# A two-layer decoder trunk on one core: the k-tiles of tokens and of z moved from 2048 to 2080 bytes apart

## The chip, the cores and the metric

The kernel runs as one launch on one core of a Trainium2 chip. The metric is the device time of that launch in microseconds. Three runs of the kernel before took 821.86, 821.97 and 822.0 us; the median is 821.97 us.

## The reference

Two layers work on a sequence of 256 positions (T) of width 2048 (D). Everything that costs time is a product with a large fp32 weight matrix:

```python
for i in range(2):
    if i == 1:
        k_blocks, v_blocks, k_mean = moba_shared_kv(h, w_kv_shared)   # h @ (2048 x 3072)
    u = h @ w_in[i]                                                    # 2048 x 4096
    branch_in, gate_b, mem_q, gate_m = jnp.split(u, split_at, axis=-1)
    branch = multiscale_pool(...) if i == 0 else moba_attention(...)
    mem_o = memory_attention(mem_q, mem, w_mem_kv[i])                  # mem @ (2048 x 1024), 4 heads
    mixed = jnp.concatenate([branch * silu(gate_b), mem_o * silu(gate_m)], -1)
    h = layer_norm(DEEPNORM_ALPHA * h + mixed @ w_out[i], ln_g[i], ln_b[i])
```

The sequence is one attention block long, so the attention of layer 1 is plain causal attention over 12 heads of 128.

## The kernel before, in words

Each fp32 operand is held as two fp32r parts, a high one and a low one (`split`, L69 to L72: ScalarE copies to the high part, VectorE subtracts to get the low part). A product is high x high + high x low + low x high. All matmuls go through `mm` (L66, L67), so nearly all of them carry L67 in the profile, and they are told apart by the names of their tiles. In the profile's names the tile before the comma or after it may be either operand; which one streams (moving) and which one is loaded into the array (weights of the array, "stationary") is told here.

The activations stand transposed, with the 2048 channels cut into 16 k-tiles of 128 partitions. One k-tile of a transposed activation is 512 numbers per partition: 256 positions of the high part, then 256 of the low part, 2048 bytes in all. Three such tensors stay in the on-chip memory: `xT` (the tokens, later the output of layer 0), `memT` (the memory tokens) and `zT` (the gated branches, "z"). `xT` and `memT` lie in one large tile `xm`, `memT` right behind `xT`, both moved up by `SHIFT` = 40 numbers (160 bytes) from the start of the tile (L55 to L57). `zT` is a tile of its own that begins with its first k-tile (L59).

Weight matrices arrive as 128 x 1024 blocks (`raw`, 4 buffers) on SP's DMA queue, and each is split into `wh` and `wl` (4 buffers each, 4096 bytes per partition). A list of items, one for each block, is worked off in order by `run` (L130 to L164): at item i the block i+4 is loaded, the block i+3 is split, and the matmuls of item i are issued. There are two forms of projection.

`proj_t` (L167 to L191) makes a transposed result. The weight block is the array's operand, in slices of 128 numbers (512 bytes), and the k-tile of `xT` or `memT` streams past it: 512 columns against the slice of `wh`, then 256 columns (the high part alone) against the slice of `wl`. For each k-tile there is thus one pair of matmuls.

`proj_n` (L193 to L217) makes a result with positions on the partitions. Here 128 positions of the k-tile are the array's operand, and 512 columns of the weight block stream: the high part against `wh`, the high part against `wl`, the low part against `wh`. It is used for the memory values (`mem_v`, with `memT`), the shared values (`w_sv`, with `xT`) and the output projections (`out_0`, `out_1`, with `zT`).

Some weight blocks are split into parts of `xm` that are no longer needed. The blocks of `w_sv` go to where `memT` stood (`in_mem`, L650), so they too begin 160 bytes into a multiple of 512. The last 512 columns of the second output projection go to `kept` (L58), which is laid over `xm` without the shift, and `last` (L731) multiplies `zT` by them: 512 columns for the first 128 positions, twice 256 columns for the others. `pool_mix` (L563) streams 256 columns of `zT` past slices of a small weight block.

The addresses modulo 512 bytes follow from the shapes. `xm` (66,048 bytes per partition), `zT`, `res`, `raw`, `wh` and `wl` all have sizes that are multiples of 512 and stand behind one another, and slices of the weight blocks begin at multiples of 512 in them. Take the distance as the start of what streams minus the start of the array operand that is loaded during it, modulo 512 bytes. Before the change it is 160 in `proj_t`, 352 in `mem_v` (the array operand is 160 ahead), and 0 in `w_sv`, the output projections, `last` and `pool_mix`.

The results of `proj_t` for heads and gates pass through a small tile `fold` (L223 to L245, 3 buffers): ScalarE copies one half of the sum, VectorE adds the other, and the tile is free when VectorE's L229 (heads) or L242 (gates, one item later) has read it.

Of the kernel before, what the change touches and what calls it, by code (L numbers as in the profile page):

```python
# [11 lines left out]
F32 = mybir.dt.float32  # L12
F32R = mybir.dt.float32r
# [4 lines left out]
P = 128  # L18
T = 256
D = 2048  # L20
KT = D // P
# [11 lines left out]
BLK = 1024  # L33
RAW_BUFS = 4
WARM = 10
SHIFT = 40
W_BUFS = 4
SHIFT = 40
LD = 4
LEAD = 3  # L40
LD0 = 8
# [4 lines left out]
def trunk(ctx: ExitStack, tc: tile.TileContext, a: dict, out: bass.AP):  # L46
    nc = tc.nc
    ctx.enter_context(tc.manual_schedule())
    sb = ctx.enter_context(tc.tile_pool(name="sb", bufs=1))
# [2 lines left out]

    xm = sb.tile([P, 2 * KT * 2 * T + 128], F32R, name="xm")  # L55
    KX = KT * 2 * T
    xT, memT = (xm[:, SHIFT + i * KX:SHIFT + (i + 1) * KX].rearrange("p (k t) -> p k t", k=KT) for i in range(2))  # L57
    kept = [xm[:, i * KX:(i + 1) * KX].rearrange("p (k n) -> p k n", k=KT) for i in range(2)]  # L58
    zT = sb.tile([P, KT, 2 * T], F32R, name="zT")  # L59
    res = sb.tile([P, 2, D], F32, name="res")  # L60
    ident = mask = psc = eps_t = stats = None

# [29 lines left out]
    def later(n, fn):  # L92
        events[now[0] + n].append(fn)
# [6 lines left out]
    def load(it):  # L100
        for c0, c1 in zip(it["cuts"], it["cuts"][1:]):
            load_piece(it, c0, c1)
# [15 lines left out]
    def prep(it):  # L118
        for c0, c1 in zip(it["cuts"], it["cuts"][1:]):
            prep_piece(it, c0, c1)  # L120
# [9 lines left out]
    def run():  # L130
# [15 lines left out]
        for i in range(n):  # L146
            now[0] = i
            if i + LP < n:
                prep(items[i + LP])
            if LD0 <= i + LD < n:  # L150
                load(items[i + LD])
            it = items[i]
# [66 lines left out]
    def fold(dst, acc):  # L219
        nc.scalar.activation(dst, acc[:, T:], AF.Copy)  # L220
        nc.vector.tensor_add(dst, acc[:, :T], dst)  # L221

    def to_heads(dst, base):  # L223
        def done(n, acc):
            s = sb.tile([P, T], F32, name="fold", bufs=3)
            hi, lo = dst()[:, base + n, :T], dst()[:, base + n, T:]
            fold(s, acc)
            nc.vector.tensor_copy(hi, s)
            nc.vector.tensor_sub(lo, s, f(hi))  # L229
        return done  # L230

    def to_gate(dst, base):

        def done(n, acc):
            s = sb.tile([P, T], F32, name="fold", bufs=3)
            fold(s, acc)
            g = dst()

            def finish():
                th = sb.tile([P, T], F32, name="th", bufs=2)  # L240
                nc.scalar.activation(th, s, AF.Tanh, scale=0.5)
                nc.vector.scalar_tensor_tensor(g[:, base + n, :], th, 1.0, s,  # L242
                                               op0=ALU.add, op1=ALU.mult)
            later(1, finish)
        return done  # L245
# [6 lines left out]
    def heads_tile(name):  # L252
        return sb.tile([P, 4, 2 * T], F32R, name=name)
# [202 lines left out]
    def fresh(key, make):  # L456

        tiles = []

        def g():  # L460
            if not tiles:
                tiles.append(make())
                st[key] = tiles[0]
            return tiles[0]
        return g
# [183 lines left out]

    def in_mem(j):  # L650

        return [memT[:, 4 * (j % 4) + 2 * i:4 * (j % 4) + 2 * i + 2].rearrange("p k n -> p (k n)") for i in range(2)]

    mem_q_gate(1)
    for grp in range(3):
        k = fresh("k", lambda: heads_tile("kk"))
        q = fresh("q", lambda: heads_tile("qq"))
        g = fresh("g", gate_tile)
        v = fresh("v", val_tile)
        for c in range(2):  # L660
            proj_t(xT, [a["w_sk"][2 * grp + c, kb] for kb in range(4)], to_heads(k, 2 * c))
        for c in range(2):
            proj_t(xT, w_in(1, 2 * grp + c), to_heads(q, 2 * c))
        prs = [MobaPair(2 * j, 4 * grp + 2 * j, st) for j in range(2)]

        def go(prs=prs):
            plan(prs[0], 1, 5, 17)
            plan(prs[1], 7, 18, 20)
        after(go)
        for c in range(2):  # L670
            proj_t(xT, w_in(1, 6 + 2 * grp + c), to_gate(g, 2 * c))
        proj_n(xT, [a["w_sv"][grp, kb] for kb in range(8)], to_values(v), place=in_mem)
# [189 lines left out]
```

## Time and profile before

| | us |
|---|---|
| median of 3 runs | 821.97 |
| profiled execution, its own time | 822.53 |
| its span, first to last instruction | 820.8 |
| PE busy (matmul) | 810.8 |
| PEld busy (weight load) | 700.9 |
| DVE busy | 558.5 |
| ACT busy | 396.2 |

The page's 40 slices show PE at nine tenths or more in every slice but the last, and the granted TensorE clock the same way (mean 0.995 of full speed). A busy PE is not a PE at its peak: matmuls overlap, so the mean time of one is longer than the distance from one start to the next. The distance between starts is what adds up to the span, and it is read from the timeline.

### The profile page before, as it was taken

What the parts mean: (1) busy time and instruction counts of PE and PEld (TensorE: products, weight loads), DVE (VectorE), ACT (ScalarE), POOL (GpSimd) and SP (SyncE); (2) the same over time, 40 slices, a digit from 0 to 9 for tenths busy, and PEclk for the clock granted to TensorE, in tenths of its full rate; (3) what the DMA queues carried; (4) which work ended last, traced back from release to release, by engine and by line L of the source; (5) the groups of instructions that cost most, each with busy time, mean ns of one, the idle gap of its engine ahead of it and who ended that gap; (6) DMA issues with size and microseconds to landing.
All of it is one profiled execution on the core that took longest, in us unless ns stands there. A gap on an engine that the chain in (4) does not pass through costs nothing.

```text
span 820.8 us, 11537 instructions
## 1 busy us (share of the span) xinstructions
PE 810.8 (99%) x4446; PEld 700.9 (85%) x4446; DVE 558.5 (68%) x794; ACT 396.2 (48%) x578; POOL 0.2 (0%) x4
## 2 busy tenths in 40 slices
PE   9999999999999999999999999999999999999996
PEld 6888888898888888888888888888888888888885
DVE  5786678657956555797667667576765667658746
ACT  6564545545545343545455445354554445545520
POOL 0000000000000000000000000000000000000000
PEclk9999999999999999999999999999999999999998
DMA  8876545456557655676554544645455554636742
GB/s 319 298 250 206 170 154 192 172 181 212 185 190 278 221 186 199 201 234 201 185 170 143 193 162 163 212 159 189 177 173 170 185 187 158 224 113 233 277 132 103
DMA packets 47164, 159.15 MB, mean 194 GB/s; under 512 B 5375, under 2 KB 7167, under 8 KB 46847
## 3 DMA queue, kind: packets, MB, share of 16 engines
q1 hardware_dynamic: 45792, 155.21, 56.3%
q10 hardware_dynamic: 1316, 3.19, 1.0%
q8 instruction: 35, 0.57, 0.3%
q14 instruction: 21, 0.17, 0.1%
HBM read 156.28 MB, written 2.10 MB: 193 GB/s over the span
## 4 chain that ended last, share of the span: by engine, by line
PE 98%; DVE 1%; DMA 1%; SPq 0%; ACT 0%; issue 0%; DVEq 0%
PE acc L67 89%; PE o L67 4%; PE s L67 2%; PE pt L67 2%; DMA raw<-in_w_mk 1%; PE pt L362 0%; PE pt L312 0%; SPq L98 0%; DVE res L805 0%; PE o L637 0%; PE pt L637 0%; DVE res L786 0%; DVE wl L72 0%; ACT wh L71 0%; DVE stats L744 0%
## 5 line engine op out<-in xcount | busy, mean ns | idle before, releaser
L67 PE MATMUL acc<-xm,wh 128*128 128x512 f32 x1344 | 466.8, 394 | 0.5 <-ACT wh L71 0.5
L72 DVE TENSOR_TENSOR wl<-raw,wh 128x1024 fp32r<-128x1024 f32 (+2 forms) x250 | 295.0, 1187 | 149.8 <-ACT wh L71 148.8
L67 PE MATMUL acc<-xm,wl 128*128 128x256 f32 x1344 | 362.6, 280 | 0.1
L71 ACT ACTIVATE wh<-raw 128x1024 fp32r<-128x1024 f32 (+2 forms) x250 | 255.5, 1028 | 188.5 <-PE acc L67 131.2
L67 PEld LDWEIGHTS acc<-xm,wh 128*128 128x128 f32 x1344 | 247.2, 188 | 49.1 <-ACT wh L71 1.0
L67 PEld LDWEIGHTS acc<-xm,wl 128*128 128x128 f32 x1344 | 252.7, 188 | 7.9 <-DVE wl L72 0.9
L67 PE MATMUL acc<-wh,zT 128*128 128x512 f32 x448 | 140.0, 390 | 0.0
L67 PEld LDWEIGHTS acc<-wh,zT 128*128 128x128 f32 x448 | 84.1, 188 | 17.3
L67 PE MATMUL acc<-wl,zT 128*128 128x512 f32 x224 | 87.2, 389 | 0.0
L67 PE MATMUL acc<-xm 128*128 128x512 f32 x288 | 65.8, 389 | 0.0
L67 PEld LDWEIGHTS acc<-xm 128*128 128x128 f32 x288 | 54.1, 188 | 11.2
L72 DVE TENSOR_TENSOR xm<-raw,xm 128x1024 fp32r<-128x1024 f32 (+2 forms) x41 | 47.8, 1171 | 21.1 <-ACT xm L71 21.1
L220 ACT ACTIVATE fold<-acc 128x256 f32<-128x256 f32 x72 | 27.7, 385 | 60.8 <-PE acc L67 59.6
L71 ACT ACTIVATE xm<-raw 128x1024 fp32r<-128x1024 f32 (+2 forms) x41 | 41.3, 1014 | 19.1 <-PE acc L67 9.8
L67 PEld LDWEIGHTS acc<-wl,zT 128*128 128x128 f32 x224 | 42.1, 188 | 8.5
L221 DVE TENSOR_TENSOR fold<-acc,fold 128x256 f32<-128x256 f32 x72 | 29.5, 419 | 4.6 <-ACT fold L220 4.6
L71 ACT ACTIVATE zT<-zf 128x256 fp32r<-128x256 f32 x32 | 12.9, 414 | 39.6 <-DVE zf L282 35.4
L67 PE MATMUL acc<-xm,zT 128*128 128x256 f32 (+1 forms) x144 | 22.6, 318 | 0.0
L67 PEld LDWEIGHTS acc<-xm,zT 128*128 128x128 f32 x144 | 20.7, 190 | 1.9
L67 PE MATMUL acc<-wh,xm 128*128 128x512 f32 x64 | 21.6, 403 | 0.0
L71 ACT ACTIVATE ph<-pt 128x384 fp32r<-128x384 f32 (+1 forms) x20 | 10.7, 535 | 22.2 <-PE pt L362 13.5
L72 DVE TENSOR_TENSOR zT<-zf,zT 128x256 fp32r<-128x256 f32 x32 | 12.9, 423 | 9.7 <-ACT zT L71 9.7
(124 smaller groups left out, 504.4 us busy)
## 6 DMA issues: line engine op xcount, KB each, us to landing
raw<-in_w_in SPq DMA_DIRECT2D x128, 512.0 KB, 3.5
raw<-in_w_out SPq DMA_DIRECT2D x64, 512.0 KB, 4.1
raw<-in_w_sk SPq DMA_DIRECT2D x24, 512.0 KB, 4.4
raw<-in_w_sv SPq DMA_DIRECT2D x24, 512.0 KB, 3.3
raw<-in_w_mv SPq DMA_DIRECT2D x14, 512.0 KB, 5.2
raw<-in_w_mk SPq DMA_DIRECT2D x12, 512.0 KB, 3.4
raw<-in_xT SPq DMA_DIRECT2D x4, 512.0 KB, 4.8
res<-in_x ACTq DMA_DIRECT2D x2, 1024.0 KB, 5.4
```

The lines of the kernel that those rows point to most:

```text
L67: nc.tensor.matmul(o, l, r, start=start, stop=stop)
L71: nc.scalar.activation(hi, src, AF.Copy)
L72: nc.vector.tensor_sub(lo, src, f(hi))
L220: nc.scalar.activation(dst, acc[:, T:], AF.Copy)
L221: nc.vector.tensor_add(dst, acc[:, :T], dst)
```

## The change

The k-tiles of `xT`, `memT` and `zT` are `KP` = 520 numbers (2080 bytes) apart, with 8 unused numbers behind each. The start of k-tile k thus moves on by 32 bytes modulo 512 with each k, so the 16 k-tiles begin at the 16 multiples of 32 bytes. `xm` grows by 1024 bytes per partition, `zT` by 512. `in_mem` is given its own view, `inmem`, of unbroken 4096-byte blocks that begins where `memT` begins; `kept` stays. Both uses of `fold` get 2 buffers in place of 3. A second definition of `SHIFT` goes.

```diff
-SHIFT = 40
 W_BUFS = 4
 SHIFT = 40
+KP = 2 * T + 8
...
-    xm = sb.tile([P, 2 * KT * 2 * T + 128], F32R, name="xm")
     KX = KT * 2 * T
-    xT, memT = (xm[:, SHIFT + i * KX:SHIFT + (i + 1) * KX].rearrange("p (k t) -> p k t", k=KT) for i in range(2))
+    xm = sb.tile([P, 2 * KX + 384], F32R, name="xm")
+    at = [SHIFT + i * KT * KP for i in range(2)]
+    xT, memT = (xm[:, c:c + KT * KP].rearrange("p (k t) -> p k t", k=KT)[:, :, :2 * T] for c in at)
+    inmem = xm[:, at[1]:at[1] + KX].rearrange("p (b n) -> p b n", n=BLK)
     kept = [xm[:, i * KX:(i + 1) * KX].rearrange("p (k n) -> p k n", k=KT) for i in range(2)]
-    zT = sb.tile([P, KT, 2 * T], F32R, name="zT")
+    zT = sb.tile([P, KT, KP], F32R, name="zT")[:, :, :2 * T]
...
     def to_heads(dst, base):
...
-            s = sb.tile([P, T], F32, name="fold", bufs=3)
+            s = sb.tile([P, T], F32, name="fold", bufs=2)
...
     def to_gate(dst, base):
...
-            s = sb.tile([P, T], F32, name="fold", bufs=3)
+            s = sb.tile([P, T], F32, name="fold", bufs=2)
...
     def in_mem(j):
...
-        return [memT[:, 4 * (j % 4) + 2 * i:4 * (j % 4) + 2 * i + 2].rearrange("p k n -> p (k n)") for i in range(2)]
+        return [inmem[:, 2 * (j % 4) + i] for i in range(2)]
```

## Rows read from the trace of the kernel before

**Rows 1.** The page's first part: busy time of each engine, share of the span, instructions.

```profile
span 820.8 us, 11537 instructions
PE 810.8 (99%) x4446; PEld 700.9 (85%) x4446; DVE 558.5 (68%) x794; ACT 396.2 (48%) x578; POOL 0.2 (0%) x4
```

**Rows 2.** The page's fourth part: the chain of work that ended last, its shares of the span by engine and by line.

```profile
PE 98%; DVE 1%; DMA 1%; SPq 0%; ACT 0%; issue 0%; DVEq 0%
PE acc L67 89%; PE o L67 4%; PE s L67 2%; PE pt L67 2%; DMA raw<-in_w_mk 1%; PE pt L362 0%; PE pt L312 0%; SPq L98 0%; DVE res L805 0%; PE o L637 0%; PE pt L637 0%; DVE res L786 0%; DVE wl L72 0%; ACT wh L71 0%; DVE stats L744 0%
```

**Rows 3.** The groups of instructions, shapes kept apart, PE's matmuls: line, engine, operation, tiles, shape, count | busy us, mean ns of one | idle before. `xm,wh` and `xm,wl` are `proj_t`; `wh,zT` and `wl,zT` the output projections; `xm` alone is `w_sv`; `wh,xm` and `wl,xm` (on acc, pt and o) are `mem_v`; `xm,zT` is `last`.

```profile
L67 PE MATMUL acc<-xm,wh 128*128 128x512 f32 x1344 | 466.8, 394 | 0.5 <-ACT wh L71 0.5
L67 PE MATMUL acc<-xm,wl 128*128 128x256 f32 x1344 | 362.6, 280 | 0.1
...
L67 PE MATMUL acc<-wh,zT 128*128 128x512 f32 x448 | 140.0, 390 | 0.0
L67 PE MATMUL acc<-wl,zT 128*128 128x512 f32 x224 | 87.2, 389 | 0.0
...
L67 PE MATMUL acc<-xm 128*128 128x512 f32 x288 | 65.8, 389 | 0.0
...
L67 PE MATMUL acc<-wh,xm 128*128 128x512 f32 x64 | 21.6, 403 | 0.0
...
L67 PE MATMUL acc<-wl,xm 128*128 128x512 f32 x32 | 12.6, 393 | 0.0
L67 PE MATMUL acc<-xm,zT 128*128 128x256 f32 x96 | 11.7, 283 | 0.0
...
L67 PE MATMUL pt<-wh,xm 128*128 128x512 f32 x32 | 11.4, 396 | 0.0
L67 PE MATMUL o<-wh,xm 128*128 128x512 f32 x32 | 11.4, 396 | 0.0
L67 PE MATMUL acc<-xm,zT 128*128 128x512 f32 x48 | 11.0, 389 | 0.0
...
L67 PE MATMUL pt<-wl,xm 128*128 128x512 f32 x16 | 6.3, 394 | 0.0
L67 PE MATMUL o<-wl,xm 128*128 128x512 f32 x16 | 6.3, 393 | 0.0
```

**Rows 4.** The chain in order of time: start us, length us, what it ran, with the count of matmuls. Two stretches of `proj_t`.

```profile
17.55 5.56 PE acc L67 x32
...
411.16 11.12 PE acc L67 x64
```

**Rows 5.** The timeline of PE at the start of a `proj_t` stretch: start us, length us, instruction.

```profile
411.00 0.39 PE L67 MATMUL acc<-xm,wh 128*128 128x512 f32 x1
411.23 0.28 PE L67 MATMUL acc<-xm,wl 128*128 128x256 f32 x1
411.35 0.39 PE L67 MATMUL acc<-xm,wh 128*128 128x512 f32 x1
...
413.78 0.39 PE L67 MATMUL acc<-xm,wh 128*128 128x512 f32 x1
```

**Rows 6.** The timeline of PE over two items of `mem_v` in layer 0, 24 matmuls, and the first matmul behind them.

```profile
22.94 0.39 PE L67 MATMUL pt<-wh,xm 128*128 128x512 f32 x1
23.17 0.39 PE L67 MATMUL pt<-wl,xm 128*128 128x512 f32 x1
23.40 0.63 PE L67 MATMUL pt<-wh,xm 128*128 128x512 f32 x2
...
28.30 0.39 PE L67 MATMUL o<-wh,xm 128*128 128x512 f32 x1
28.53 0.39 PE L67 MATMUL acc<-xm,wh 128*128 128x512 f32 x1
```

**Rows 7.** The timeline of PE over the 96 matmuls of `w_sv` for the first group of heads, and the first matmul behind them.

```profile
506.69 21.95 PE L67 MATMUL acc<-xm 128*128 128x512 f32 x96
528.48 0.39 PE L67 MATMUL acc<-xm,wh 128*128 128x512 f32 x1
```

**Rows 8.** The timeline of PE in the first output projection; 16 matmuls begin from the start of the first row up to the start of the last.

```profile
299.95 0.39 PE L67 MATMUL acc<-wl,zT 128*128 128x512 f32 x1
300.18 0.62 PE L67 MATMUL acc<-wh,zT 128*128 128x512 f32 x2
...
303.58 0.62 PE L67 MATMUL acc<-wh,zT 128*128 128x512 f32 x2
```

**Rows 9.** Sums by stretch: busy time and count of each engine, granted TensorE clock (the number before the DMA share), DMA share, GB/s. A stretch of `mem_v`, of the output projection and of `proj_t`.

```profile
23.00:28.50 5.50, 5.50 (x25) 4.46 (x25) 2.71 (x4) 2.12 (x2) 0.00 (x0) 1.00 0.91 346
262.00:336.00 74.00, 74.00 (x329) 61.26 (x328) 42.55 (x44) 30.96 (x30) 0.00 (x0) 1.00 0.61 200
411.00:422.00 11.00, 11.00 (x65) 9.65 (x64) 7.58 (x13) 6.83 (x14) 0.00 (x0) 1.00 0.44 150
```

**Rows 10.** The timeline of ACT: the third and the fourth of the four `fold` tiles of layer 0's memory keys, the ones that follow most closely on the tile two before them.

```profile
44.06 0.39 ACT L220 ACTIVATE fold<-acc 128x256 f32<-128x256 f32 x1
45.45 0.39 ACT L220 ACTIVATE fold<-acc 128x256 f32<-128x256 f32 x1 [1.01 <-DVE wl L72]
```

**Rows 11.** The timeline of DVE at the same place: the last readings of the first and of the second of these tiles.

```profile
42.46 0.43 DVE L229 TENSOR_TENSOR kk<-fold,kk 128x256 fp32r<-128x256 f32 x1
43.86 0.43 DVE L229 TENSOR_TENSOR kk<-fold,kk 128x256 fp32r<-128x256 f32 x1
```

## The prediction

> **What bounds the kernel.** I read the busy times first: PE is busy for 810.8 of 820.8 us, the next engine, DVE, for 558.5 [rows 1]. The chain that ended last is PE for 98%, and 89% of the span are the large projections at L67 [rows 2]. The groups then show that PE hardly waits: 0.5 us of idle time in front of the 1344 wide `proj_t` matmuls, none in front of the others [rows 3]. So the time is the number of matmuls times the distance from one start to the next, and a change that touches only addresses can act in two ways: it alters that distance, or it makes some buffer late enough to stop PE.
>
> The distances come from the timeline. In `proj_t` eight pairs take 413.78 - 411.00 = 2.78 us, 347.5 ns a pair [rows 5]; the chain gives the same, 11.12 us for 32 pairs and 5.56 us for 16 [rows 4]. In the output projection 16 matmuls take 303.58 - 299.95 = 3.63 us, 227 ns each [rows 8]; in `w_sv` 96 take 528.48 - 506.69 = 21.79 us, 227 ns [rows 7]; in `mem_v` 24 take 28.53 - 22.94 = 5.59 us, 233 ns [rows 6]. In the 256-column half of `last`, whose matmuls follow one another directly, 95 steps and one whole matmul make 11.7 us: (11.7 - 0.28) / 95 = 120 ns [rows 3]. All this runs at a granted clock of 1.00 [rows 9], the 2.4 GHz level, at which 512 columns are 213 ns and 256 are 107. So each matmul pays about 13 ns beyond its columns, and the ones of `mem_v` 20.
>
> What differs between `mem_v` and the output projection? Both are `proj_n`, with the same shapes and the same order; what streams is a weight block in both. The distance between what streams and the array operand loaded meanwhile is 352 bytes modulo 512 in the one and 0 in the other. `w_sv` again is the same form, with the same activation tile `xm` as array operand and as the target of the splits, and it has distance 0 and 227 ns. I take this as the sign that the distance does cost something. The mean length of one matmul agrees: 389 to 390 ns for 512 columns at distance 0, 394 at 160, 393 to 403 at 352 [rows 3].
>
> **What the change does to it.** It takes no instruction away and adds none. After it, the distance in `proj_t` is 160 + 32k, in `mem_v` 352 - 32k, in `w_sv` and the output projections -32k, in `pool_mix` 32k, all modulo 512, with k from 0 to 15 (0 to 11 in `pool_mix`). Each large projection goes through all sixteen k once for each result, so each then pays the mean over sixteen distances in place of the price of one. Three of the sixteen are priced by rows. Against distance 0 a 512-column matmul pays nothing at 0 and 233 - 227 = 6 ns at 352. At 160 only the pair is sure: 347.5 against 227 + 120 = 347 at distance 0, 0.5 ns more; by the lengths the wide one pays some 4 ns more (394 against 389 to 390) and the narrow one 3 less (280 against 283), which nearly cancel.
>
> For the unknown thirteen the bounds are the dearest and the cheapest rows. Above: in `mem_v` the first of each three is the dearest, at 403 ns a length on acc against 389 at distance 0, 14 ns more. If every wide matmul paid that, the 1344 of `proj_t` would pay 9 more than now (403 against 394, +12.1 us), the 1008 that now stand at distance 0 (448 + 224 + 288 + 48) 14 more (+14.1 us); with the narrow ones back at 283 (+4.0 us) the total is +30 us. Below: every wide matmul of `proj_t` at 389.5 as at distance 0 (1344 x -4.5 = -6.0 us), the narrow ones kept at 280, the 192 of `mem_v` at 227 (-1.2 us): -7 us. That is the floor if no unseen distance is cheaper than the seen ones; it need not hold (below).
>
> The value I take gives each of the sixteen the price of the nearest priced one, around the circle: five lie nearest to 0, five and a half each to 160 and 352. With 0, 4 and 6 ns the mean is (5.5 x 4 + 5.5 x 6) / 16 = 3.4 ns for a wide matmul. `proj_t`: from 4 to 3.4, 1344 x -0.6 = -0.8 us. The 1008 from 0 to 3.4: +3.4 us. `mem_v`: from 6 to 3.4, 192 x -2.6 = -0.5 us. The narrow half of `proj_t` now has -3 at 160; with 0 at 0, and 0 assumed at 352, which no row shows for 256 columns, its mean is 5.5 x -3 / 16 = -1.0, so 1344 x 2.0 = +2.7 us. The 96 narrow ones of `last` and some 108 of `pool_mix` gain 1.0 each, -0.2 us. Sum: -0.8 + 3.4 - 0.5 + 2.7 - 0.2 = +4.6 us. The prices are rounded to the ns and the shift of 4 and 3 ns inside a pair is a reading of lengths, whose ends are modelled; I take +4.
>
> The Trainium skill speaks against any such cost. "SBUF — State Buffer", section "Who interferes with whom", gives PE two independent read ports, one for the moving operand and one for the weight load, and says that PE never waits on anyone. By that rule the sum is 0. The 233 against 227 ns of two stretches of one form [rows 6, 8] is not explained by it, so it is a rival below and not the forecast.
>
> **The other edits.** `fold` with 2 buffers: a third tile must wait until the first is read. At the closest place the first is read out at 42.46 + 0.43 = 42.89 and the third is written at 44.06, the second is read out at 44.29 and the fourth written at 45.45 [rows 10, 11]: 1.2 us of room, so the wait costs nothing. If it did wait, ACT would stand, and behind it the splits of later blocks, which are made three items (some 8 us at 2.78 each) ahead of PE. `inmem` still begins 160 bytes into a multiple of 512 and holds the same blocks. The overlap of `kept` with the shifted tokens concerns tokens that were last read items earlier. Splits into `xT` and `zT` write the same rows in other places, on ACT and DVE, which PE does not wait for [rows 3]; their cover is the 262 us that DVE has free [rows 1]. I price all these at nothing.
>
> **The result.** The profiled execution took 822.53 us, 1.7 us more than its span; plus 4 it is 826.5. It lies 0.56 above the median of the runs, so the forecast for the median is 826.0.
>
> **Rivals.**
> - *The distance is no cause.* The 6 ns of `mem_v` come from something else in it, for instance from the memory tokens being split while it runs in layer 0. Against it: `w_sv` too runs beside splits into `xm` and holds 227 ns [rows 7]. For it: 160 and 0 differ by only 0.5 ns a pair. The time is then 822.0, unchanged. Chance 0.22. (The port rule of the Trainium skill, "SBUF — State Buffer", "Who interferes with whom", would give the same.)
> - *Not slower: unseen distances are cheaper.* 13 ns beyond the columns may be itself a toll that the fixed distances pay and others don't; all rows stand at three distances only. The narrow matmul, 3 ns shorter at 160 than at 0, speaks for it: a distance can be cheaper than 0. Against it: no wide matmul in any group is shorter than 389 ns [rows 3]. It decides as soon as the mean of the wide ones over the sixteen distances falls below that of now. At the narrow one's gain, -3 ns from the price at 0 on all of them: `proj_t` 1344 x -7 = -9.4, the 1008 -3.0, `mem_v` 192 x -9 = -1.7 us, together -14 and a time of 808. Half of that, 815, is the time I give it, for some of the sixteen will be dear as 352 is. Chance 0.26.
> - *The dear distances are the rule.* 352 is no exception, and the steps with distances from about 256 up behave like the first of three in `mem_v`. Half the way to the upper bound is +15 us, 837. Chance 0.10.
>
> **Chances and range.** Forecast (+2 to +10 us) 0.42, no effect 0.22, faster 0.26, much slower 0.10. A measurement of this kernel tells about 0.2%, 1.6 us, from no change. The forecast and the third rival are slower by more than that; of the rival with cheaper distances nearly all is faster by more: faster 0.27, same 0.22, slower 0.51. The range from 811 to 836 leaves out the far end of the second rival (about 0.1) and most of the third. Within the likeliest case alone it is 824 to 832.
>
> **What would show it.** Right: the starts of the wide matmuls in the output projection, all 227 ns apart now, differ from k to k, with a mean of 230 or so; `mem_v` falls below 233; pairs of `proj_t` differ from k to k around 349; PE's idle time stays as it is. The first rival: all distances stay at 227, 347.5 and 233. The second: output projection below 227 in the mean. If PE gets new idle time with ACT's `fold` or a split as what ended it, the price of the other edits was wrong. The forecast is wrong if the mean pair in `proj_t`, half of all the time, moves by more than 3 ns either way: each ns there is 1.3 us.

## The result: 1.0% slower

Four runs of the changed kernel took 830.45 to 830.63 us, median 830.49; the kernel before, beside them on the same chip, 821.99. The ratio is 1.0101 (95% interval 1.0084 to 1.0119). The prediction said slower, at 826.0 us: the sign and the place were right and the size half of what came, +8.5 us in place of +4. The profiled execution of the changed kernel took 830.5 us with a span of 828.6, so 7.8 of the 8.5 us are in the two spans compared here. One run of one experiment below (tokens alone, 893.18 us at a granted clock of 0.849) was slow as a whole and is left out of its median.

First the busy times of the changed kernel, to set against [rows 1]:

```profile
span 828.6 us, 11557 instructions
PE 818.4 (99%) x4446; PEld 701.2 (85%) x4446; DVE 558.7 (67%) x794; ACT 395.9 (48%) x578; POOL 0.2 (0%) x4
```

Then PE's groups, with the columns of [rows 3]. The line numbers of this kernel are 2 higher, so L69 is `mm`.

```profile
L69 PE MATMUL acc<-xm,wh 128*128 128x512 f32 x1344 | 470.1, 396 | 0.3 <-ACT wh L73 0.3
L69 PE MATMUL acc<-xm,wl 128*128 128x256 f32 x1344 | 363.1, 280 | 0.2 <-DVE wl L74 0.2
L69 PE MATMUL acc<-wh,zT 128*128 128x512 f32 x448 | 142.3, 395 | 0.0
L69 PE MATMUL acc<-wl,zT 128*128 128x512 f32 x224 | 88.1, 393 | 0.0
L69 PE MATMUL acc<-xm 128*128 128x512 f32 x288 | 67.4, 394 | 0.0
L69 PE MATMUL acc<-wh,xm 128*128 128x512 f32 x64 | 21.6, 403 | 0.0
```

PE grew by 7.6 us, and DVE and ACT stayed where they were. PE waits no more than before: 0.5 us of idle time over the 2688 matmuls of `proj_t`, and 4.4 us at the two ends of the program, in both kernels. So nothing came late; the same matmuls follow one another more slowly. The mean length tells where: the output projections went from 390 and 389 ns to 395 and 393, `w_sv` from 389 to 394, the wide ones of `proj_t` from 394 to 396; the narrow ones of `proj_t` and `mem_v` hardly moved.

The timeline of PE shows it as distances between starts: two items of `mem_v`, to set against [rows 6], a stretch of the output projection, against [rows 8], two items of `proj_t` (16 pairs), against [rows 5], and `w_sv` for the first group of heads, against [rows 7].

```profile
22.98 0.40 PE L69 MATMUL pt<-wh,xm 128*128 128x512 f32 x1
...
28.56 0.39 PE L69 MATMUL acc<-xm,wh 128*128 128x512 f32 x1
...
299.77 0.63 PE L69 MATMUL acc<-wh,zT 128*128 128x512 f32 x2
300.24 0.40 PE L69 MATMUL acc<-wl,zT 128*128 128x512 f32 x1
300.48 0.62 PE L69 MATMUL acc<-wh,zT 128*128 128x512 f32 x2
300.93 0.39 PE L69 MATMUL acc<-wl,zT 128*128 128x512 f32 x1
...
303.25 0.63 PE L69 MATMUL acc<-wh,zT 128*128 128x512 f32 x2
...
489.24 0.39 PE L69 MATMUL acc<-xm,wh 128*128 128x512 f32 x1
...
494.85 0.40 PE L69 MATMUL acc<-xm,wh 128*128 128x512 f32 x1
...
510.90 22.46 PE L69 MATMUL acc<-xm 128*128 128x512 f32 x96
533.20 0.39 PE L69 MATMUL acc<-xm,wh 128*128 128x512 f32 x1
```

`w_sv`: (533.20 - 510.90) / 96 = 232.3 ns, 227 before. Output projection: 15 matmuls from 299.77 to 303.25, 3.48 us, 232 ns each, and no longer even: two of the same kind take 0.47 us at 299.77 and 0.45 us at 300.48. `mem_v`: 5.58 us for 24, 232.5 ns against 233. `proj_t`: 16 pairs from 489.24 to 494.85, 5.61 us, 351 ns a pair against 347.5.

Added up over the whole trace, from each start to the next, the two kernels compare so:

| matmuls | before, us | after, us | change |
|---|---|---|---|
| `proj_t`, 1344 pairs | 469.9 | 473.6 | +3.7 |
| output projections, 672 | 152.9 | 156.3 | +3.4 |
| `w_sv`, 288 | 65.3 | 66.9 | +1.6 |
| `mem_v`, 192 | 45.3 | 45.1 | -0.2 |
| `last`, 144 | 25.4 | 25.5 | +0.1 |
| everything else, 461 | 55.3 | 54.4 | -0.9 |

The sum is +7.7 us, nearly all of the span's 7.8. Half of the last line has nothing to do with the change: the steps between the last three matmuls are 0.45 us shorter, since the granted clock was 0.50 there in the trace of before and 0.97 in that of the changed kernel. The rest lies in the warm-up, the pool mix and the last normalisation.

The wide half of `last` shows that no other engine has to take part. Nothing but PE works in these stretches, the first of the kernel before, the second of the changed one (columns as in [rows 9]; DVE, ACT, POOL and DMA stand at 0):

```profile
791.60:798.90 7.30, 7.30 (x34) 6.05 (x33) 0.00 (x0) 0.00 (x0) 0.00 (x0) 1.00 0.00 0
800.00:807.30 7.30, 7.30 (x33) 5.94 (x32) 0.00 (x0) 0.00 (x0) 0.00 (x0) 1.00 0.00 0
```

From start to start these matmuls take 226 to 227 ns before the change and 226 to 237 after it; over all 48 of them the mean goes from 226.7 to 231.5 ns. So the splits and the loads of weight blocks, which run beside all the other projections, are not what slows them.

### The profile page after: what moved, and what is told of

The parts are those of the page before. It is cut to its first block, busy times and chain, and to the rows that moved or that the text cites. A ratio compares the mean times of both kernels' runs of the same rounds, so it can differ in the third digit from the quotient of the medians.

```text
span 828.6 us, 11557 instructions
## 1 busy us (share of the span) xinstructions
PE 818.4 (99%) x4446; PEld 701.2 (85%) x4446; DVE 558.7 (67%) x794; ACT 395.9 (48%) x578; POOL 0.2 (0%) x4
## 4 chain that ended last, share of the span: by engine, by line
PE 98%; DVE 1%; DMA 1%; SPq 0%; ACT 0%; issue 0%; DVEq 0%
PE acc L69 89%; PE o L69 4%; PE s L69 2%; PE pt L69 2%; DMA raw<-in_w_mk 1%; PE pt L364 0%; PE pt L314 0%; SPq L100 0%; PE pt L639 0%; PE o L639 0%; DVE res L807 0%; DVE res L788 0%; DVE wl L74 0%; DVEq L860 0%; ACT wh L73 0%
## 5 line engine op out<-in xcount | busy, mean ns | idle before, releaser
L69 PE MATMUL acc<-xm,wh 128*128 128x512 f32 x1344 | 470.1, 396 | 0.3 <-ACT wh L73 0.3
L69 PE MATMUL acc<-xm,wl 128*128 128x256 f32 x1344 | 363.1, 280 | 0.2 <-DVE wl L74 0.2
L69 PEld LDWEIGHTS acc<-xm,wh 128*128 128x128 f32 x1344 | 247.5, 188 | 50.7 <-ACT wh L73 1.0
L69 PEld LDWEIGHTS acc<-xm,wl 128*128 128x128 f32 x1344 | 253.4, 189 | 8.8 <-DVE wl L74 1.0
L69 PE MATMUL acc<-wh,zT 128*128 128x512 f32 x448 | 142.3, 395 | 0.0
L69 PEld LDWEIGHTS acc<-wh,zT 128*128 128x128 f32 x448 | 84.1, 188 | 19.5
L69 PE MATMUL acc<-wl,zT 128*128 128x512 f32 x224 | 88.1, 393 | 0.0
L69 PE MATMUL acc<-xm 128*128 128x512 f32 x288 | 67.4, 394 | 0.0
L69 PEld LDWEIGHTS acc<-xm 128*128 128x128 f32 x288 | 54.1, 188 | 12.7
L69 PEld LDWEIGHTS acc<-wl,zT 128*128 128x128 f32 x224 | 42.1, 188 | 9.6
L69 PE MATMUL acc<-xm,zT 128*128 128x256 f32 (+1 forms) x144 | 22.6, 318 | 0.0
L69 PEld LDWEIGHTS acc<-xm,zT 128*128 128x128 f32 x144 | 20.5, 188 | 2.2
L69 PE MATMUL acc<-wh,xm 128*128 128x512 f32 x64 | 21.6, 403 | 0.0
```

The source lines that it names most:

```text
L69: nc.tensor.matmul(o, l, r, start=start, stop=stop)
```

## The experiments

The theory is called D below: the distance modulo 512 bytes between what streams and the array operand that is loaded meanwhile sets how closely matmuls follow one another. All times are medians, and ratios are against the kernel before on the same chip. That it is the load during the streaming that counts is argued and not shown; what the runs can show is that the distance of the two operands does.

**The pitch undone, the rest kept.** The first question was whether the other edits had any part in it.

```diff
-KP = 2 * T + 8
+KP = 2 * T
```

> The changed kernel with KP = 512 numbers again: k-tiles 2048 bytes apart, but fold still with 2 buffers, inmem still a view of its own and xm still of the larger size. Theory D (the distance between what streams and the array operand loaded meanwhile costs PE time): all distances are again 160 in proj_t, 352 in mem_v, 0 elsewhere, so the time is that of the kernel before, 822.0 us, with 227 ns from start to start in the output projection. Rival E (the other edits, such as the lost fold buffer, cost the time): it stays at 830 us.

Measured: 822.23 us beside 822.14, ratio 1.0002 (0.9992 to 1.0011). Its chain over a stretch of `proj_t`, and then the timeline of its `w_sv`:

```profile
484.96 11.12 PE acc L69 x64
```

```profile
506.33 21.95 PE L69 MATMUL acc<-xm 128*128 128x512 f32 x96
528.11 0.39 PE L69 MATMUL acc<-xm,wh 128*128 128x512 f32 x1
```

32 pairs in 11.12 us as in [rows 4], and (528.11 - 506.33) / 96 = 226.9 ns as in [rows 7]. The second `fold` buffer, `inmem` and the larger `xm` cost nothing; rival E falls.

**The two halves, one at a time.** Tokens and memory tokens alone:

```diff
-    zT = sb.tile([P, KT, KP], F32R, name="zT")[:, :, :2 * T]
+    zT = sb.tile([P, KT, 2 * T], F32R, name="zT")
```

> Only the k-tiles of the tokens and of the memory tokens (xT, memT) are 2080 bytes apart, those of z 2048. Theory D, with the sums of starts read from the two traces: proj_t +3.8 us, w_sv +1.6, mem_v -0.2, so +5.1 and about 827 us; the output projections stay at 227 ns. Rival E (other edits): 830 us.

Measured: 827.08 us, the median of three, ratio 1.0061 (1.0044 to 1.0077). And z alone:

```diff
-    at = [SHIFT + i * KT * KP for i in range(2)]
-    xT, memT = (xm[:, c:c + KT * KP].rearrange("p (k t) -> p k t", k=KT)[:, :, :2 * T] for c in at)
+    XP = 2 * T
+    at = [SHIFT + i * KT * XP for i in range(2)]
+    xT, memT = (xm[:, c:c + KT * XP].rearrange("p (k t) -> p k t", k=KT)[:, :, :2 * T] for c in at)
```

> Only the k-tiles of z are 2080 bytes apart. Theory D: the 672 matmuls of the output projections go from 227.5 to 232.6 ns, +3.4 us, so about 825.5 us; proj_t stays at 347.5 ns a pair. With the run on the tokens alone it adds up to the whole (+8.5 us). Rival E (other edits): 830 us.

Measured: 825.52 us, ratio 1.0041 (1.0027 to 1.0056). +4.9 and +3.4 us add up to 8.3 of the 8.5. Each kernel has slowed down exactly where its own distances changed. For tokens alone, the timeline of `w_sv` and the group of the output projection:

```profile
508.88 22.46 PE L69 MATMUL acc<-xm 128*128 128x512 f32 x96
531.18 0.39 PE L69 MATMUL acc<-xm,wh 128*128 128x512 f32 x1
```

```profile
L69 PE MATMUL acc<-wh,zT 128*128 128x512 f32 x448 | 139.9, 390 | 0.0
```

For z alone, the same:

```profile
508.34 21.95 PE L70 MATMUL acc<-xm 128*128 128x512 f32 x96
530.13 0.39 PE L70 MATMUL acc<-xm,wh 128*128 128x512 f32 x1
```

```profile
L70 PE MATMUL acc<-wh,zT 128*128 128x512 f32 x448 | 142.3, 395 | 0.0
```

With the tokens moved, `w_sv` is at 232.3 ns and the output projection at its old 390 ns of length; with z moved it is the other way round, 227.0 ns and 395.

**All distances at 0.** If 0 is the cheapest distance, the kernel before should gain from it in `proj_t` too.

```diff
-SHIFT = 40
+SHIFT = 0
```

> The kernel before with SHIFT = 0: every distance is 0 modulo 512 bytes, in proj_t and mem_v too. Theory D with 0 as the cheapest distance: mem_v goes from 233 to 227 ns (192 matmuls, -1.2 us), a pair of proj_t from 347.5 to 347 ns (-0.7 us): about 820 us. Rival F (a pair of a wide and a narrow matmul behaves otherwise at 0 than rows of one width show): proj_t grows, and the time is above 822 us.

Measured: 827.38 us, ratio 1.0064 (1.0049 to 1.0079). The expectation of D failed, rival F holds. Two groups, and the timeline of two items of `mem_v`:

```profile
L66 PE MATMUL acc<-xm,wh 128*128 128x512 f32 x1344 | 472.5, 399 | 0.0
...
L66 PE MATMUL acc<-wh,xm 128*128 128x512 f32 x64 | 21.4, 400 | 0.0
```

```profile
22.92 0.40 PE L66 MATMUL pt<-wh,xm 128*128 128x512 f32 x1
...
28.39 0.39 PE L66 MATMUL acc<-xm,wh 128*128 128x512 f32 x1
```

`mem_v` did what was expected: 24 matmuls in 5.47 us, 228 ns in place of 233. But the wide matmuls of `proj_t` are now 399 ns long in place of 394, and a pair takes 354.0 ns on the whole-trace mean, 349.6 in the kernel before. A wide matmul behind a wide one is cheap at distance 0 and a narrow one behind a narrow one takes 120 ns there; in turns the two are dear.

**Distance or place.** In the changed kernel the k-tiles also begin at new places, some at odd multiples of 32 bytes. Moving everything leaves the distances alone and changes every place.

```diff
+    sb.tile([P, 8], F32, name="first")
     xm = sb.tile([P, 2 * KT * 2 * T + 128], F32R, name="xm")
```

> The kernel before with 32 bytes reserved in front of everything: xm, zT and the weight tiles all begin 32 bytes later, so every address changes and no distance does. Theory D (what counts is the distance between what streams and the array operand): 822.0 us, 347.5 ns a pair in proj_t, 227 ns in the output projection, 233 in mem_v, as before. Rival A (what counts is where a k-tile itself begins, and in the changed kernel those that begin at odd multiples of 32 bytes are dear): the weights and z now begin at such a place, the output projection goes to 233 to 234 ns and the time up by 4 us or more.

Measured: 822.34 us, ratio 1.0002 (0.9993 to 1.0012). Chain and timeline:

```profile
485.05 11.12 PE acc L67 x64
```

```profile
506.41 21.95 PE L67 MATMUL acc<-xm 128*128 128x512 f32 x96
528.19 0.39 PE L67 MATMUL acc<-xm,wh 128*128 128x512 f32 x1
```

347.5 ns a pair and 226.9 ns, as before the move. The place doesn't count, and rival A falls. The traces hold no addresses: that the new tile moves the others by 32 bytes follows from the order and the sizes of the tiles, and the runs below show the same without it.

**One distance for all k-tiles at a time.** Six kernels give the kernel before other constant distances, by `SHIFT` for the tokens and by a shift of the whole of z. The first is shown; in the second the two numbers are 64 and 64, in the third 8 and 96.

```diff
-SHIFT = 40
+SHIFT = 16
...
-    zT = sb.tile([P, KT, 2 * T], F32R, name="zT")
+    zT = sb.tile([P, KX + 128], F32R, name="zT")[:, 120:120 + KX].rearrange("p (k t) -> p k t", k=KT)
```

In the third the blocks of `w_sv` also stay where they were, 160 bytes into a multiple of 512, so that its distance is 128.

> The kernel before with constant distances: 32 in the output projections (z moved by 480 bytes as a whole), 64 in proj_t and 448 in mem_v (SHIFT = 16 numbers), 0 in w_sv. Theory P (each distance has a price that holds whatever the distance of the matmul before): with the means of the changed kernel's trace the output projection goes to 233.5 ns (+4.4 us), a proj_t pair to 346 ns (-1.7 us): about 825 us. Rival N (the price hangs on the distance of the neighbours too): the output projection at constant 32 or the pair at constant 64 differ from these by more than 2 ns. Rival A (where a tile begins): as P for z, but proj_t unchanged.

> The kernel before with constant distance 256 in proj_t, mem_v, the output projections and last; w_sv stays at 0. If the price repeats every 256 bytes, the output projection and mem_v stand at 227 ns and a proj_t pair at 351 as with all distances at 0: about 827 us. Theory P with the means of the changed kernel's trace: output projection 230 ns (+2.0 us), pair 347 (-0.9 us), mem_v 229 (-0.8 us): about 822.5 us.

> The kernel before with constant distances 32 in proj_t, 480 in mem_v, 128 in w_sv, the output projections and last. Theory P with the means of the changed kernel's trace: output projection 230.6 ns (+2.4 us), w_sv 230.4 (+1.0 us), proj_t pair 349 (+2.4 us), mem_v 233: about 828 us. Rival N: one of these off by more than 2 ns.

Measured: 831.79 us (ratio 1.0114, 1.0097 to 1.0131), 827.27 us (1.0064, 1.0049 to 1.0079) and 827.61 us (1.0066, 1.0051 to 1.0081). The groups of the first and of the second, then chain and timeline of the third:

```profile
L66 PE MATMUL acc<-xm,wh 128*128 128x512 f32 x1344 | 472.7, 397 | 0.0
L66 PE MATMUL acc<-xm,wl 128*128 128x256 f32 x1344 | 364.7, 281 | 0.0
L66 PE MATMUL acc<-wh,zT 128*128 128x512 f32 x448 | 142.6, 396 | 0.0
```

```profile
L66 PE MATMUL acc<-xm,wh 128*128 128x512 f32 x1344 | 472.5, 399 | 0.1
L66 PE MATMUL acc<-wh,zT 128*128 128x512 f32 x448 | 139.8, 390 | 0.0
```

```profile
487.18 11.13 PE acc L66 x64
```

```profile
508.56 22.47 PE L66 MATMUL acc<-xm 128*128 128x512 f32 x96
530.87 0.39 PE L66 MATMUL acc<-xm,wh 128*128 128x512 f32 x1
```

At 32 the output projection stands at 233.6 ns, as theory P had it. But the pair at 64 is at 353.9 ns in place of 346: the price that a distance shows among changing neighbours is not the one it has when all are alike, so P falls and N holds. At 256 all is as at 0 (390 and 399 ns of length in both): the price at 256 bytes is that at 0, and P's 822.5 us is wrong. In the third, `w_sv` at 128 takes (530.87 - 508.56) / 96 = 232.4 ns, 2.0 more than P said, and the pair at 32 takes 11.13 / 32 = 347.8 ns, the first constant as cheap as 160.

From these I drew a rule (R), by which a pair is cheap at odd multiples of 32 bytes and dear at even ones, and wide matmuls that follow one another are cheap at 0 and 256 alone, and put it to the test with three more kernels of the same kind, with `SHIFT` and the shift of z at 24 and 112, at 32 and 124, and at 56 and 0:

```diff
-SHIFT = 40
+SHIFT = 24
...
-    zT = sb.tile([P, KT, 2 * T], F32R, name="zT")
+    zT = sb.tile([P, KX + 128], F32R, name="zT")[:, 112:112 + KX].rearrange("p (k t) -> p k t", k=KT)
```

> The kernel before with constant distance 96 in proj_t (SHIFT = 24 numbers, 416 in mem_v) and 64 in the output projections. Theory R, from the runs so far: wide matmuls that follow one another cost 227 ns at 0 and 256 and 232 to 233.5 everywhere else; a proj_t pair costs 347.5 ns at odd multiples of 32 and 352 at even ones. Then the pair stays at 347.5, the output projection goes to 232 to 233.5 ns (+3.3 to 4.1 us): 825.5 to 826 us. Against it: an output projection at 64 at 230 or below, a pair at 96 more than 2 ns away from 347.5.

> Constant distance 128 in proj_t (384 in mem_v) and 16 in the output projections. Theory R: the pair at 352 ns (+6 us), mem_v at 232 to 233; if only exact multiples of 256 are cheap, the output projection at 16 is at 232 to 233.5 ns (+3.3 to 4.1 us): 831 to 832 us. If the cheap place is wider than 16 bytes, it stays at 227 ns: 828 us.

> Constant distance 224 in proj_t (288 in mem_v), all others at 0 as before. Theory R: a pair at 347.5 ns as at the other odd multiples of 32, mem_v at 233, so 822 us, the time of the kernel before. A pair more than 2 ns away from that (2.7 us in the time) would mean that odd and even is not the rule.

Measured: 827.35 us (ratio 1.0059, 1.0044 to 1.0074), 827.07 us (1.0054, 1.0037 to 1.0071) and 828.67 us (1.0073, 1.0058 to 1.0088). The chain over a `proj_t` stretch of the first and the second, and the group of the third:

```profile
488.60 11.23 PE acc L66 x64
```

```profile
488.73 11.22 PE acc L66 x64
```

```profile
L66 PE MATMUL acc<-xm,wh 128*128 128x512 f32 x1344 | 473.5, 398 | 0.0
```

Rule R falls: the pair is at 11.23 / 32 = 350.9 ns at 96, where R said 347.5, and no dearer at 128 (350.6), and the group at 224 is as dear as at 0. The output projection stands at 229.5 ns at 64 and at 228.8 at 16, below what R gave. All constants together, each a mean over the whole trace, from start to start, with the longer steps at the edges of blocks in it (160 stands at 349.6 here and at 347.5 between edges):

| distance, bytes | output projection, ns each | `proj_t`, ns a pair |
|---|---|---|
| 0 | 227.5 | 354.0 |
| 16 | 228.8 | |
| 32 | 233.6 | 349.9 |
| 64 | 229.5 | 353.9 |
| 96 | | 352.7 |
| 128 | 232.6 | 353.2 |
| 160 | | 349.6 |
| 224 | | 354.3 |
| 256 | 227.4 | 354.2 |
| all sixteen, the change | 232.6 | 352.4 |

These kernels speak against rival A a second time. `SHIFT` moves the tokens and the blocks of `w_sv` together, so the distance of `w_sv` stays 0 wherever both begin. At 0, 64, 96, 128, 160, 224 and 256 bytes into a multiple of 512 (the kernel before and that with all distances at 0 among them) its mean over the whole trace lies between 226.7 and 227.2 ns. In the third of the six kernels, with the tokens at 32 and the blocks left at 160, it is 232.4.

**A kernel that beats both.** Only `mem_v` stood at a dear distance in the kernel before. Its weight blocks can be split into z's tile, which is idle then, at the place that gives distance 0.

```diff
-    zT = sb.tile([P, KT, 2 * T], F32R, name="zT")
+    zs = sb.tile([P, KX + 128], F32R, name="zT")
+    zT = zs[:, :KX].rearrange("p (k t) -> p k t", k=KT)
...
-        proj_n(memT, [a["w_mv"][layer, kb] for kb in range(8)], to_values(v), banks=banks)
+        proj_n(memT, [a["w_mv"][layer, kb] for kb in range(8)], to_values(v), banks=banks,
+               place=lambda j: [zs[:, SHIFT + (2 * (j % 4) + i) * BLK:SHIFT + (2 * (j % 4) + i + 1) * BLK] for i in range(2)])
```

> The kernel before with one distance changed: the weight blocks of mem_v are split into z's tile, which is unused at that time, 160 bytes into a multiple of 512, so that mem_v too has distance 0; proj_t stays at 160 and all others at 0. From the runs so far: the 192 matmuls of mem_v go from 233 to 227 ns, -1.2 us, everything else stays: about 820.8 us, 0.15% below the kernel before, about what a comparison of five rounds can just tell. Rival N (the price of a distance hangs on more than the distance of this form): mem_v stays at 230 ns or more and the time at 822 us.

Measured: 821.56 us beside 822.31, ratio 0.9990 (0.9981 to 0.9999). The timeline of the same two items of `mem_v`:

```profile
22.98 1.55 PE L67 MATMUL pt<-zT,xm 128*128 128x512 f32 x6
...
28.45 0.39 PE L67 MATMUL acc<-xm,wh 128*128 128x512 f32 x1
```

24 matmuls of `mem_v` in 5.47 us, 228 ns, against 5.59 us in [rows 6]. It is faster than both kernels, by 0.1% against the kernel before, with an interval that just keeps clear of 1. It gained 0.8 us of the 1.2 that were expected: over the whole trace the matmuls of `mem_v` go from 45.3 to 44.5 us, to 228 ns each in layer 0 and from 238 only to 235 in layer 1, where the first step of each item stays longer (294 ns on the mean, 299 before).

## Why the prediction was half right

**What bounds the kernel** held. PE's idle time is between 4.4 and 5.0 us in every one of these kernels, and the whole change is in the distance from start to start.

**The distance as the cause** held. It was read from one difference, 233 against 227 ns in two stretches of one form. The runs show it from four sides: undoing the pitch gives the time back, each half costs where it lies, moving everything costs nothing, and moving `mem_v` alone to distance 0 gives 5 ns back in layer 0. The first rival, no effect at all, is out. With it falls, for this case, what was drawn from the Trainium skill, "SBUF — State Buffer", section "Who interferes with whom": PE has two read ports there, independent of one another, and the sum was to be 0 by that, while the runs show up to 6.1 ns a matmul that hang on the addresses of the two operands. The trace does not say what PE waits on: the weight loads keep their mean length (188 to 189 ns in `proj_t` and the output projection, before and after).

**The other edits at nothing** held, by the first experiment.

**The price of the thirteen unseen distances** is the step that failed: each of the sixteen was given the price of the nearest of three, which made 3.4 ns for a wide matmul against distance 0. The two groups that stood at 0 paid more: the output projections 5.1 ns (227.5 to 232.6), `w_sv` 5.4, together 5.0 us where the 1008 were to pay 3.4 us. The guess took 0 for the middle of a broad cheap stretch. It is a narrow one, met again at 256: 16 bytes away the output projection pays 1.3 ns more, 32 bytes away 6.1, 64 bytes away 2.0. The price doesn't rise evenly with the distance, so the nearest priced row was no guide.

**`proj_t`** was to pay 1.9 us, -0.8 in the wide matmuls and +2.7 in the narrow ones; it paid 3.7. The split was wrong as well as the sum: by starts, the wide ones went from 231.9 to 234.8 ns and the narrow ones from 117.7 to 117.6. Here the forecast took 160 for a distance like the others. It is one of the two cheapest of the eight constants tried, so any spread had to lose: the sixteen together give 352.4 ns, near the dear constants. By its own sign the forecast was wrong if the mean pair moved by more than 3 ns; it moved by 2.8.

**`mem_v`** was to gain 0.5 us and gained 0.2.

The terms make 4.6 us where 7.7 came. The second rival (cheaper unseen distances) found no support in the output projection, where no mean below 227 ns turned up. The third (as dear as the first matmul of each three in `mem_v`, 14 ns above distance 0) went too far: no class of the table is more than 7 ns above its cheapest constant. Its 403 ns were misread: the 64 matmuls of that row are the first and the third of each three in layer 1, and the mean is raised by the first of each item, 460 ns long on the mean; in layer 0 the first of each three is 398 ns.

## What to carry to other kernels

Where PE is the bound and its matmuls follow one another without a wait, measure start to start by group, not busy time: matmuls of equal shape at 227 and at 233 ns are worth a question. If the addresses of the two operands differ in that, try constant distances one by one, separately for each form of matmul, since the best one differed (0 modulo 256 where wide ones follow wide ones, 32 or 160 where wide and narrow take turns). Giving every tile its own distance bought something like a mean here (352.4 ns a pair, where the eight constants run from 349.6 to 354.3), and that was a loss because the constants in use were among the cheap ones.

## What was not expected of the hardware

The price of a distance hangs on the sequence. At distance 0 a wide matmul behind a wide one takes 227 ns and a narrow one behind a narrow one 120 ns, 347 together, but in turns a pair takes 351 to 352 ns between blocks' edges and 354.0 with them (all distances at 0). In the changed kernel, matmuls of the output projection whose own distance is 0 start 224 to 237 ns apart, 230.7 on the mean (the first of each block left out), not 227. And the narrow matmuls of `last`, at 120 ns at 0, took 113 ns with z at constant distance 64, less than at any other constant:

```profile
L66 PE MATMUL acc<-xm,zT 128*128 128x256 f32 x96 | 11.0, 276 | 0.0
```

(11.0 - 0.28) / 95 = 113 ns. That is the kernel with pairs at 96. Why the price at 256 bytes is that at 0, and why the turns of wide and narrow change the order of the distances, stays open: the traces show when matmuls start and not what holds them, and no run here takes the weight load away from under a streaming matmul.
